# Input projection: the row loads of token blocks 0 and 1 ordered behind the last block's fifth row on ScalarE's queue

## The chip, the cores and the metric

The kernel runs on one core of a Trainium2 chip. The metric is the device time of one execution in microseconds (us); lower is better. Five engines work from queues of their own, each in order: TensorE (PE, matmuls), VectorE (DVE), ScalarE (ACT), GpSimd (POOL) and SyncE (SP). They wait for one another by semaphores. Transfers between memory and the core's buffers run on 16 DMA engines; a transfer is issued from the queue of SP, ACT or POOL, in order with what else stands in that queue.

## The reference, cut to what matters

One layer of a streaming encoder on 1024 prompt tokens and 8 x 16 sample tokens, in float32. What the change touches is its beginning:

```python
def rms_norm(x, g):
    xf = x.astype(jnp.float32)
    y = xf * lax.rsqrt(jnp.mean(xf * xf, axis=-1, keepdims=True) + EPS)
    return (y * g.astype(jnp.float32)).astype(x.dtype)

def hybrid_layer(x, p, ...):
    xn = rms_norm(x, norm_g)                       # 2048 wide
    u, g_pool, c_q, c_kv, k_r, g_mla = jnp.split(xn @ w_in, SPLIT_IDX, axis=-1)
    ...                                            # pooling mixer, latent attention
    h = x + jnp.concatenate([pool_out, mla_out], axis=-1) @ w_out
    gate = jax.nn.sigmoid(rms_norm(h, ple_norm_g) @ w_ple_gate + b_ple_gate)
    y = h + gate * (p @ w_ple)
```

## The kernel before, in words

The 1152 tokens are three blocks of TB = 384: blocks 0 and 1, and the "last block" (block 2). The 2048 features are 16 rows of 128; a row of one block is a tile of 128 partitions x 384 (192 KB). A value is split into a high and a low float32r part (`k.split`: ScalarE writes the high part, VectorE the low one), and a product is three matmuls: high x high, low x high, high x low (L175 to L177 in this phase; L77 to L79 in others).

The input projection (`phase1`) is a sum over two halves of the features. For the last block a product with one column of weights is plain: eight rows times three matmuls, 24. `EARLY` = 26 such columns come first and need only the last block's rows X0 to X7 (tiles x0 to x7 loaded by SyncE; X0h, X0l and so on are their two halves) and weights (`wraw`, split into `wh` and `wl`). The weight buffers are three deep before the split and five deep after it.

Meanwhile `row(c)` loads row c of blocks 0 and 1, for all 16 rows, as two transfers each on ScalarE's queue (32 in all), squares it on ScalarE and adds it to R on VectorE. Rows 0 to 7 go to tiles x0 to x7 (the buffers that the last block's rows leave), rows 8 to 15 in turn to two buffers xs. When R is whole, six small matmuls (L327, tile aux) and a chain on VectorE turn it into a factor per token, the rows are normalised (L371), and `first_operands` makes the operands 11, S1, S2, S3, S4, 12 and 22 from sums and differences of them. With these the products of blocks 0 and 1 run in pairs of columns with seven products instead of eight (`Quick.pair`): its intermediate results u2 (L210), u3 (L221) and q (L226) are made on VectorE. Between the pairs `second_operands` loads the rows of the second half (tiles a0 to a3), scales them (L464), forms their sums (L384 to L391) and stores them (tensor sums), all on SyncE's queue. After the second pair the shared rope key is projected (`key`, L438), with its own weights (wh_354).

The order in which each engine's instructions stand is not the order of the code: the tile framework plays the program through a cost model of its own when it is built, and gives each engine the order in which things came out there. `tc.issue_after(ins)` adds to this that what is written in its block stands behind `ins` on the engine of `ins`. So an edit at one place can move instructions far from it.

Of the kernel before, what the change touches and what calls it, by code (L numbers as in the profile page):

```python
# [8 lines left out]
AF = mybir.ActivationFunctionType  # L9
ALU = mybir.AluOpType  # L10
# [11 lines left out]
TB = 384  # L22
# [230 lines left out]
def phase1(k, sc):  # L253
# [4 lines left out]
    tc, nc, io = k.tc, k.nc, k.io  # L258
# [30 lines left out]
    def o_tile():  # L289
        return k.t(xp, [P, TB], "o", bufs=3)  # L290
# [10 lines left out]
    def last_block(c, j):  # L301

        i = 8 * c + j
        raw = (o_tile() if c else k.t(rp, [P, 2 * TB], f"x{j}"))[:, :TB]
        nc.sync.dma_start(raw, io["xT"][2][:, i, :])
        hl = [k.t(xp, [P, TB], f"X{j}{x}", F32R) for x in "hl"]
        k.split(hl[0][:], hl[1][:], raw, k.norm_g[:, i:i + 1])
        if c == 0:
            squares(R2, raw, raw)
        return hl  # L310

    begun = set()

    def squares(acc, raw, sq):

        if id(acc) not in begun:
            begun.add(id(acc))
            nc.scalar.activation(acc[:], raw, AF.Square)
        else:
            nc.scalar.activation(sq, raw, AF.Square)  # L320
            nc.vector.tensor_tensor(acc[:], acc[:], sq, ALU.add)
# [23 lines left out]
    raw = k.t(wp, [P, 8, P], "wraw", bufs=3)  # L345
    wn = [k.t(wp, [P, 8, P], f"w{x}", F32R, bufs=5) for x in "hl"]
    X = []
    for a, b in ((0, 1), (1, 2), (2, 4), (4, 8)):
        nc.sync.dma_start(raw[:, a:b, :], src[0][:, a:b, :])
        if a == 0:  # L350
            consts(k)
        k.split(wn[0][:, a:b], wn[1][:, a:b], raw[:, a:b])
        X += [last_block(0, j) for j in range(a, b)]
# [3 lines left out]
    def row(c):  # L357

        raw = k.t(rp, [P, 2 * TB], f"x{c}" if c < 8 else "xs", bufs=1 if c < 8 else 2)
        for t in range(2):  # L360
            nc.scalar.dma_start(raw[:, t * TB:(t + 1) * TB], io["xT"][t][:, c, :])
        squares(R, raw[:], (k.t(rp, [P, 2 * TB], "sq") if c < 8 else raw)[:])
        rows.append(raw)

# [34 lines left out]
    def square_rest(i):  # L399
        raw = o_tile()  # L400
        nc.sync.dma_start(raw[:], io["xT"][2][:, i, :])
        squares(R2, raw[:], raw[:])

    steps += [lambda c=c: row(c) for c in range(16)] + [norms, normalise]
    steps += [lambda j=j: first_operands(j) for j in range(4)]
    for i in range(EARLY):
# [95 lines left out]
    for n in OPS:  # L502
        for j in range(4):
            raw = k.t(ap, [P, TB], f"a{j}")
            nc.sync.dma_start(raw[:], sc["sums"][:, 4 * OPS.index(n) + j, :])
            put(n, j, raw[:])
    hs.close()
    X = [last_block(1, j) for j in range(8)]

    def prior(i, t):  # L510
# [1053 lines left out]
def layer(tc, io):  # L1564
    k = K(tc, io)
    with tc.tile_pool(name="dram", bufs=1, space=DRAM) as dp, tc.tile_pool(name="const", bufs=1) as cp:
        sc = scratch(dp, k)
        k.cp = cp
        first = phase1(k, sc)
        next(first)  # L1570
        shared = Shared(k)
# [110 lines left out]
```

## Time and profile before

| | us |
|---|---|
| median of 3 runs (lowest to highest) | 2288.55 (2285.35 to 2288.8) |
| the profiled execution, its own time | 2292.38 |
| its span, first to last instruction | 2290.6 |
| TensorE busy in the span | 2211.1 |
| VectorE busy | 1439.5 |
| ScalarE busy | 1004.0 |
| TensorE busy from 0 to 134 us | 123.04 |
| TensorE busy from 0 to 185 us | 165.12 |
| mean granted clock of TensorE | 0.987 |

TensorE is busy for 97% of the span, so the rows to look at are those in which it stands idle or works slowly. A row of the timeline has the start, the length, engine, line, operation, output<-inputs (without buffer numbers) and, in brackets, the idle time of that engine just before and what ended it. PEld is the weight load of a matmul; SPq and ACTq are the queues that issue transfers. A row of the waits has the waiting engine and line, who was waited for, the sum in us, how often, and the longest. A row of the stretches (from:to in us) has the busy time of PE, PEld, DVE, ACT and POOL with the number of instructions, the granted clock, the DMA engines' busy share and GB/s.

### The profile page before, as it was taken

To read this page: it belongs to the slowest core of one execution; us is meant where nothing else is said; L and a number is where in the kernel's file an instruction comes from. 1 tells how busy PE (TensorE), PEld (TensorE's weight loads), DVE (VectorE), ACT (ScalarE), POOL (GpSimd) and SP (SyncE) were. 2 spreads that over 40 slices of the span, in tenths; PEclk is the share of its full clock that TensorE was granted. 3 is DMA by queue.
4 is the path that set the end of the run, shared out by engine and by line. 5 is a ranking of instruction groups with operands and counts; after the bars stand their busy time and mean duration, and the time that the engine had idled before them with its cause. 6 is when DMAs were issued, how large, how long until landed. Compare 5 with 4: busy or idle time off the path is not lost.

```text
span 2290.6 us, 36006 instructions
## 1 busy us (share of the span) xinstructions
PE 2211.1 (97%) x12856; PEld 2154.0 (94%) x12856; DVE 1439.5 (63%) x3008; ACT 1004.0 (44%) x2229; POOL 410.8 (18%) x431
## 2 busy tenths in 40 slices
PE   8989999999898989989999899999999999999999
PEld 7989999999898989989998799999999999999998
DVE  6787776686777667768888765555553345344343
ACT  6533335443333467766666644343342233232232
POOL 0000000111222101034453532221002221111110
PEclk9999999999999999999999899999999999999999
DMA  9565336557766666473221754443263333222221
GB/s 303 178 225 169 125 125 213 166 161 192 190 185 179 216 206 179 130 240 99 93 84 53 241 179 152 128 154 122 85 198 112 101 121 110 86 94 96 85 87 64
DMA packets 241012, 339.24 MB, mean 148 GB/s; under 512 B 37729, under 2 KB 185313, under 8 KB 240833
## 3 DMA queue, kind: packets, MB, share of 16 engines
q1 hardware_dynamic: 217568, 290.77, 41.3%
q0 software_dynamic: 10880, 32.41, 4.4%
q10 hardware_dynamic: 12384, 13.77, 1.9%
q8 instruction: 101, 1.65, 0.3%
q14 instruction: 79, 0.64, 0.1%
HBM read 235.74 MB, written 101.12 MB: 147 GB/s over the span
## 4 chain that ended last, share of the span: by engine, by line
PE 66%; DMA 12%; DVE 9%; issue 8%; ACT 3%; POOL 2%; SPq 0%; ACTq 0%; DVEq 0%; POOLq 0%
PE mm L78 8%; PE mm L77 8%; PE mm L79 8%; PE mm L175 5%; PE mm L176 5%; PE mm L177 5%; PE f L77 3%; PE f L79 3%; PE f L78 3%; PE k L79 2%; PE k L78 2%; PE k L77 2%; DMA u<-u 1%; PE t L1215 1%; PE pb L77 1%
## 5 line engine op out<-in xcount | busy, mean ns | idle before, releaser
L68 ACT ACTIVATE wh<-wraw 128x1024 fp32r<-128x1024 f32 (+3 forms) x207 | 150.2, 729 | 146.3 <-PE mm L177 83.8
L69 DVE TENSOR_TENSOR wl<-wraw,wh 128x512 fp32r<-128x512 f32 (+3 forms) x205 | 172.0, 842 | 66.7 <-ACT wh L68 58.8
L1538 DVE TENSOR_TENSOR ev<-mm,R 128x384 f32<-128x384 f32 x48 | 26.7, 557 | 173.9 <-PE mm L79 170.0
L1539 ACT ACTIVATE ev<-ev,gains 128x384 f32<-128x384 f32 x48 | 29.4, 612 | 224.2 <-DVE ev L1538 124.4
L71 ACT ACTIVATE wh<-wraw,gains 128x128 fp32r<-128x128 f32 x256 | 82.1, 391 | 53.0 <-ACT wh L71 31.9
L72 DVE SCALAR_TENSOR_TENSOR wl<-wraw,gains,wh 128x128 fp32r<-128x128 f32 x256 | 88.0, 390 | 18.0 <-ACT wh L71 16.9
L77 PE MATMUL k<-wkh,ch 128*128 128x448 f32 x256 | 96.1, 376 | 3.2 <-ACT ch L68 2.7
L1216 ACT ACTIVATE pth<-t 128x512 fp32r<-128x512 f32 (+2 forms) x96 | 45.5, 485 | 119.7 <-PE t L1215 117.9
L68 ACT ACTIVATE wh<-wt 128x1024 fp32r<-128x1024 f32 x60 | 63.4, 1056 | 74.0 <-PE mm L177 48.5
L78 PE MATMUL k<-wkh,cl 128*128 128x448 f32 x256 | 94.5, 369 | 0.1
L79 PE MATMUL k<-wkl,ch 128*128 128x448 f32 x256 | 94.6, 369 | 0.0
L69 DVE TENSOR_TENSOR wl<-wt,wh 128x1024 fp32r<-128x1024 f32 x60 | 73.3, 1221 | 24.8 <-ACT wh L68 24.6
L79 PE MATMUL mm<-A2l,wh 128*128 128x384 f32 x256 | 86.0, 336 | 0.0
L77 PE MATMUL mm<-A2h,wh 128*128 128x384 f32 x256 | 86.0, 336 | 0.0
L78 PE MATMUL mm<-A2h,wl 128*128 128x384 f32 x256 | 86.0, 336 | 0.0
L77 PE MATMUL mm<-A0h,wh 128*128 128x384 f32 x256 | 85.8, 335 | 0.0
L79 PE MATMUL mm<-A0l,wh 128*128 128x384 f32 x256 | 85.7, 335 | 0.0
L78 PE MATMUL mm<-A1h,wl 128*128 128x384 f32 x256 | 85.7, 335 | 0.0
L78 PE MATMUL mm<-A0h,wl 128*128 128x384 f32 x256 | 85.7, 335 | 0.0
L77 PE MATMUL mm<-A1h,wh 128*128 128x384 f32 x256 | 85.5, 334 | 0.0
L79 PE MATMUL mm<-A1l,wh 128*128 128x384 f32 x256 | 85.5, 334 | 0.0
L1510 POOL TENSOR_TENSOR R<-R,sq 128x384 f32<-128x384 f32 x45 | 46.0, 1023 | 210.3 <-ACT sq L1509 210.3
(809 smaller groups left out, 7867.2 us busy)
## 6 DMA issues: line engine op xcount, KB each, us to landing
wraw<-w_in SPq DMA_DIRECT2D x89, 512.0 KB, 4.4
part<-o SPq DMA_DIRECT2D x93, 192.0 KB, 2.5
q<-part SPq DMA_DIRECT2D x93, 192.0 KB, 3.1
wraw<-w_out SPq DMA_DIRECT2D x64, 256.0 KB, 3.3
wraw<-w_ple_gate SPq DMA_DIRECT2D x64, 256.0 KB, 3.2
ple<-ev POOLq DMA_DIRECT2D x48, 192.0 KB, 2.9
fev<-xT SPq DMA_DIRECT2D x48, 192.0 KB, 2.5
hp<-fev SPq DMA_DIRECT2D x48, 192.0 KB, 2.1
```

The source lines that it names most:

```text
L68: nc.scalar.activation(hi, src, AF.Copy)
L69: eng.tensor_tensor(lo, src, hi, ALU.subtract)
L71: nc.scalar.activation(hi, src, AF.Copy, scale=scale)
L72: eng.scalar_tensor_tensor(lo, src, scale, hi, ALU.mult, ALU.subtract)
L77: mm(out, sh, mh, start=start, stop=False)
L78: mm(out, sl, mh, start=False, stop=False)
L79: self.last = mm(out, sh, ml, start=False, stop=stop)
L175: mm(ps, sh, xh[:], start=start and j == 0, stop=False, **kw)
L176: mm(ps, sl, xh[:], start=False, stop=False, **kw)
L177: self.k.last = mm(ps, sh, xl[:], start=False, stop=j == n - 1, **kw)
L1216: nc.scalar.activation(pth[:, :n, qq], tp[:, :n, :], AF.Copy)
L1510: nc.gpsimd.tensor_tensor(acc[t][:], acc[t][:], sq[:], ALU.add)
```

## The change

In `last_block` the split is written out, and the first half of it, the activation that writes the high part, is kept in a list `lead` for each of the eight rows. In `row` both loads are issued behind `lead[4]`, which is the activation of the fifth row, X4h.

```diff
         hl = [k.t(xp, [P, TB], f"X{j}{x}", F32R) for x in "hl"]
-        k.split(hl[0][:], hl[1][:], raw, k.norm_g[:, i:i + 1])
+        g = k.norm_g[:, i:i + 1]
+        hi = nc.scalar.activation(hl[0][:], raw, AF.Copy, scale=g)
+        nc.vector.scalar_tensor_tensor(hl[1][:], raw, g, hl[0][:], ALU.mult, ALU.subtract)
         if c == 0:
+            lead.append(hi)
             squares(R2, raw, raw)
...
-        for t in range(2):
-            nc.scalar.dma_start(raw[:, t * TB:(t + 1) * TB], io["xT"][t][:, c, :])
+        with tc.issue_after(lead[4].ins):
+            for t in range(2):
+                nc.scalar.dma_start(raw[:, t * TB:(t + 1) * TB], io["xT"][t][:, c, :])
```

ScalarE's queue from its first instructions, before (xs_118 and xs_119 are the buffers of rows 8 and 9, x0_54 and x1_57 the last block's first two rows):

```order
L361 DMA xs_118_424<-xT 128x384
L285 ACT_TABLE_LOAD
L285 ACTIVATE ones_46_123<-ones_46_123 128x128
L361 DMA xs_118_424<-xT 128x384
L68 ACTIVATE wh_50_129<-wraw_49_128 128x128
L361 DMA xs_119_429<-xT 128x384 x2
L320 ACTIVATE xs_118_424<-xs_118_424 128x768
L71 ACTIVATE X0h_55_139<-x0_54_137,gains_52_132 128x384
L318 ACTIVATE R2_48_127<-x0_54_137 128x384
L68 ACTIVATE wh_50_129<-wraw_49_128 128x128
L320 ACTIVATE xs_119_429<-xs_119_429 128x768
L71 ACTIVATE X1h_58_149<-x1_57_147,gains_52_132 128x384
```

And in the changed kernel, the same queue from the first split on:

```order
L308 ACTIVATE X0h_55_139<-x0_54_137,gains_52_132 128x384
L322 ACTIVATE R2_48_127<-x0_54_137 128x384
L68 ACTIVATE wh_50_129<-wraw_49_128 128x128
L308 ACTIVATE X1h_58_149<-x1_57_147,gains_52_132 128x384
L68 ACTIVATE wh_50_129<-wraw_49_128 128x256
L308 ACTIVATE X2h_61_160<-x2_60_158,gains_52_132 128x384
L308 ACTIVATE X3h_64_168<-x3_63_166,gains_52_132 128x384
L324 ACTIVATE x1_57_147<-x1_57_147 128x384
L68 ACTIVATE wh_50_129<-wraw_49_128 128x512
L324 ACTIVATE x2_60_158<-x2_60_158 128x384
L308 ACTIVATE X4h_67_179<-x4_66_177,gains_52_132 128x384
L366 DMA x0_82_241<-xT 128x384
```

The four loads of xs and the squares of them that stood ahead of X0h and X1h are gone from here; the first load of a row of blocks 0 and 1 is now x0_82, behind X4h. The xs loads stand 27 places further on, after those of x7, and ahead of the high half of the fifth column's weights (wh_106).

The order also differs from there to the second pair, on all of PE, DVE, ACT and SP, and again in the attention (PE's places 7026 to 7977 of 12822); everywhere else the five queues stand as before. VectorE's queue at the second pair's u3 (u3_351), before:

```order
L69 TENSOR_TENSOR wl_318_1407<-wraw_309_1387,wh_317_1406 128x512
L159 TENSOR_TENSOR wt_333_1500<-wraw_330_1494,wt_333_1500 128x512
L384 TENSOR_TENSOR as_561_2851<-a2_559_2841,a3_560_2842 128x384
L69 TENSOR_TENSOR wl_332_1497<-wraw_329_1492,wh_331_1496 128x1024
L297 TENSOR_TENSOR o_346_1575<-q_328_1490,o_345_1560 128x384
L297 TENSOR_TENSOR o_347_1579<-u2_323_1439,mm_322_1426 128x384
L391 TENSOR_TENSOR a2_559_2841<-a0_557_2839,a2_559_2841 128x384
L69 TENSOR_TENSOR wl_335_1504<-wt_333_1500,wh_334_1503 128x1024
L221 TENSOR_TENSOR u3_351_1629<-mm_341_1518,s1_342_1531 128x384
```

And in the changed kernel:

```order
L69 TENSOR_TENSOR wl_332_1497<-wraw_329_1492,wh_331_1496 128x1024
L391 TENSOR_TENSOR as_512_2561<-as_512_2561,a0_508_2549 128x384
L158 TENSOR_TENSOR wt_333_1500<-wraw_330_1494,wraw_329_1492 128x512
L469 SCALAR_TENSOR_TENSOR a3_560_2842<-a3_560_2842,gains_52_132,R_47_126 128x384
L394 TENSOR_TENSOR a1_509_2550<-a1_509_2550,as_512_2561 128x384
L159 TENSOR_TENSOR wt_333_1500<-wraw_330_1494,wt_333_1500 128x512
L221 TENSOR_TENSOR u3_351_1629<-mm_341_1518,s1_342_1531 128x384
L226 TENSOR_TENSOR q_352_1631<-mm_343_1533,u3_351_1629 128x384
L246 TENSOR_TENSOR u2_344_1546<-u2_344_1546,q_352_1631 128x384
L69 TENSOR_TENSOR wl_335_1504<-wt_333_1500,wh_334_1503 128x1024
```

u3_351 stands five instructions earlier: the work on a0_557, a2_559 and as_561 (second operands of the third group) and the split wl_335 have moved behind it.

More of the change, by code (lines that the diff above doesn't have):

```diff
@@ L312, in phase1 @@
     begun = set()
+    lead = []
     def squares(acc, raw, sq):
```

## The prediction

> **What bounds the kernel now.** I read first the page's busy shares and its chain of work that ended last.
>
> ```profile
> PE 2211.1 (97%) x12856; PEld 2154.0 (94%) x12856; DVE 1439.5 (63%) x3008; ACT 1004.0 (44%) x2229; POOL 410.8 (18%) x431
> PE 66%; DMA 12%; DVE 9%; issue 8%; ACT 3%; POOL 2%; SPq 0%; ACTq 0%; DVEq 0%; POOLq 0%
> ```
>
> TensorE is the bound: 2211.1 of 2290.6 us. An edit that adds no matmul can only win from the 79.5 us in which TensorE stood still, or from matmuls at a slow clock. So I asked for TensorE's waits in the stretches where the order of instructions changes. In the first 25 us:
>
> ```profile
> PE mm L175 <- ACT X0h L71: 6.2, 1, 6.2
> PE mm L175 <- ACT X1h L71: 2.3, 1, 2.3
> PE mm L175 <- ACT X5h L71: 2.0, 1, 2.0
> PE mm L176 <- DVE wl L69: 0.4, 1, 0.4
> ```
>
> 10.9 us, nearly all behind the high halves of the last block's rows on ScalarE. ScalarE's timeline (start, length, then in brackets the idle time before and what ended it) says why these are late:
>
> ```profile
> 4.72 0.84 ACT L320 ACTIVATE xs<-xs 128x768 f32<-128x768 f32 x1 [0.62 <-DMA xs<-xT]
> 5.54 0.62 ACT L71 ACTIVATE X0h<-x,gains 128x384 fp32r<-128x384 f32 x1
> 8.44 0.84 ACT L320 ACTIVATE xs<-xs 128x768 f32<-128x768 f32 x1 [1.66 <-DMA xs<-xT]
> 9.19 0.60 ACT L71 ACTIVATE X1h<-x,gains 128x384 fp32r<-128x384 f32 x1
> 15.28 0.84 ACT L318 ACTIVATE R<-x 128x768 f32<-128x768 f32 x1 [1.90 <-DMA x<-xT]
> 16.02 0.60 ACT L71 ACTIVATE X5h<-x,gains 128x384 fp32r<-128x384 f32 x1
> ```
>
> Each late half stands directly behind a square of a row of blocks 0 and 1 (xs twice, then R<-x), and two of the three squares waited over 1.6 us for their row. SyncE's queue is held too:
>
> ```profile
> SPq L305 <- DMA xs<-xT: 1.4, 1, 1.4
> 3.97 0.33 SPq L305 DMA_DIRECT2D x<-xT  x1
> x<-xT SPq DMA_DIRECT2D x8, 192.0 KB, 4.8
> ```
>
> The second row of the last block went out at 3.97 us, 1.4 us of that a wait for an xs load; such a row takes a median of 4.8 us to land. The other stretch whose order changes is that of the first pairs (125 to 185 us):
>
> ```profile
> PE mm L175 <- DVE u L221: 4.6, 1, 4.6
> PE mm L438 <- DVE wh L69: 3.6, 1, 3.6
> DVE a L464 <- DMA a<-xT: 5.6, 5, 2.5
> ```
>
> There VectorE is the bound. It waits in turn for the a loads of the second half's operands.
>
> **The change, part by part.** *Split written out* (L71 and L72 become L308 and L309): the same activation and the same scalar_tensor_tensor in the same order. Nothing.
>
> *Row loads behind the fifth row.* Before, six of the 32 issues stood ahead of X4h (four xs, two x0), and with them the three squares quoted. Now all of them come after X4h, the squares of xs after those of x1 to x6. X0h gains the 5.54 - 4.72 = 0.8 us of a square, X1h the wait of 2.3 us, X5h that of 2.0 us: 5.1 us. The lower end is set by the rows' own landing: issued at 3.97 - 1.4 = 2.6 us, the second row lands at 7.4 with the median, and X1h comes 9.19 - 7.4 = 1.8 us earlier; the same for X5h, 3.6 us in all. The upper end is 5.1 + 1.4 = 6.5 us, if SyncE's wait goes too and every later row moves up with it.
>
> What is late next are the weights. The moved loads meet them: four loads of 192 KB that had gone out first of all now lie on ScalarE's queue after x7, and the high half of the fifth column's weights (wh_106) stands behind four more issues in that in-order queue. Its cover before:
>
> ```profile
> 29.27 1.05 ACT L68 ACTIVATE wh<-wraw 128x1024 fp32r<-128x1024 f32 x1
> 30.35 1.22 DVE L69 TENSOR_TENSOR wl<-wraw,wh 128x1024 fp32r<-128x1024 f32 x1
> 34.03 0.33 PE L176 MATMUL mm<-X0h,wl 128*128 128x384 f32 x1
> 10.00:15.00 5.00, 4.65 (x12) 3.19 (x12) 4.37 (x9) 3.38 (x8) 0.00 (x0) 1.00 0.99 308
> ```
>
> The low half was done at 31.57 us and used at 34.03: 2.5 us of cover, with the DMA engines at 0.99 of their time (the last two columns are the DMA share and GB/s). TensorE wants these weights 5.1 us earlier. The path gets earlier too, since its buffers are freed earlier, but 768 KB at 308 GB/s is 2.6 us of transfer that now lies ahead of it. So 5.1 - 2.5 = 2.6 us must come from the earlier start; it lacks between 0 and 2.6. I take 0.6, near the lower end, because SyncE's own loads run alone for the first 10 us. **Start: 5.1 - 0.6 = 4.5 us, between 1.0 (3.6 - 2.6) and 6.5.**
>
> The Trainium skill, "DMA: Bandwidth & Descriptors", section "Issuing engines are not separate DMA queues", says that transfers issued by ScalarE and SyncE run on the same 16 engines and interleave. By that alone the 768 KB are only moved, and the start would be worth 5.1 - 2.6 = 2.5 us; the 0.99 above agrees with it.
>
> *The sum of squares R.* Its last addition moves later against TensorE's columns, and its six matmuls (L327) from the twelfth column to the thirteenth.
>
> ```profile
> 61.91 0.96 DVE L321 TENSOR_TENSOR R<-R,xs 128x768 f32<-128x768 f32 x1 [0.20 <-ACT xs L320]
> 66.26 1.23 PE aux L327 x12
> ```
>
> R was ready at 62.87 us and read at 66.26: 3.4 us of cover. TensorE comes 4.5 us sooner, but the reader stands 13 matmuls of 0.174 us, 2.3 us, later. Cover left if R keeps its time: 1.2 us. So nothing, and up to 2 us of loss if the loads fall behind.
>
> *The pairs.* This is the scheduler's doing, not the edit's: from 125 to 185 us four engines stand in another order. TensorE's longest wait is for the vector result u3_351, its next for the key weights wh_354.
>
> ```profile
> 154.17 1.22 DVE L69 TENSOR_TENSOR wl<-wraw,wh 128x1024 fp32r<-128x1024 f32 x1
> 155.31 0.55 DVE L297 TENSOR_TENSOR o<-q,o 128x384 f32<-128x384 f32 x1
> 157.84 0.55 DVE L221 TENSOR_TENSOR u<-mm,s 128x384 f32<-128x384 f32 x1
> 158.31 0.61 DVE L464 SCALAR_TENSOR_TENSOR a<-a,gains,R 128x384 f32<-128x384 f32 x1
> 158.84 0.55 DVE L386 TENSOR_TENSOR as<-as,a 128x384 f32<-128x384 f32 x1
> 167.29 0.69 DVE L69 TENSOR_TENSOR wh<-wraw,wh 128x512 fp32r<-128x512 f32 x1
> 171.75 0.62 DVE L464 SCALAR_TENSOR_TENSOR a<-a,gains,R 128x384 f32<-128x384 f32 x1 [2.51 <-DMA a<-xT]
> ```
>
> From the stretch's first L158 on, the new order has the same instructions ahead of u3_351 less five: two L464, L384, L391 and one weight split. By the distances between starts above (0.53, 0.47 and 1.14 us) that is 2 x 0.53 + 2 x 0.47 + 1.14 = 3.1 us. Ahead of wh_354 it has five fewer too: three L464, L386, L389, 3 x 0.53 + 2 x 0.47 = 2.5 us. The second decides when TensorE goes on, so work alone gives 2.5 us. The a loads that go later also take waits with them: 5.6 - 2.5 = 3.1 us of VectorE's waits for them lay ahead of wh_354. If all go it is 5.6 us, if half, 4.1. I take 4.0: the loads ahead of u3_351 are now two fewer of eleven, and on SyncE's queue the others stand behind fewer stores of sums. It can come out at nothing or below: all 16 operand groups still have to be done before the pair after the keys, so what is put off can be asked for at that pair, and a worse fit of SyncE's loads would cost another wait like the longest one, 4.6 us. **Pairs: 4.0 us, between -4 and +6.**
>
> *The attention stretch.* Between 1310 and 1460 us the scheduler's order differs again, with the same instructions.
>
> ```profile
> 1300.00:1350.00 50.00, 47.61 (x291) 44.20 (x290) 39.26 (x81) 31.67 (x71) 24.48 (x21) 0.98 0.79 254
> 1350.00:1400.00 50.00, 50.00 (x320) 48.48 (x319) 28.16 (x62) 20.79 (x45) 12.59 (x10) 1.00 0.44 136
> ```
>
> TensorE is busy 50.00 of 50 us from 1350 on, with VectorE at 28, so there is little to win or lose: 0, between +2.4 (the idle time of the first row) and -3. Everywhere else the four engines and GpSimd's queue stand as before, so a shift is carried to the end.
>
> **Sum.** 4.5 + 4.0 + 0 = 8.5 us. The profiled execution took 2292.38 us (span 2290.6), 3.8 above the median of the runs, 2288.55. The sum is made against its rows; I take it off the median: 2280.0 us, -0.37%. About 0.2% (4.6 us) is what a measurement of this kernel tells from no change.
>
> **The rivals.** *One of the two gains is eaten.* Either the weights behind the row loads take the start back to 1 us, or VectorE's order is worth nothing at the pairs because the work put off is wanted right after. Then 1.0 + 2.5 (VectorE's work alone) or 4.5 + 0, some 3 to 4.5 us, taken at 3.5: 2285. For it: the DMA share of 0.99 from 10 us. Against: after 21 us no wait of TensorE for weights is left to grow before the pairs. Chance 0.27; a third of it lies beyond 4.6 us.
>
> *Slower: VectorE stops at results of TensorE.* In the new order u2_323 (L210) stands ahead of three weight splits (wl_305, wl_307, wl_311), where it stood behind them, and the two results after it (u3_327, q_328) are moved forward too. Where VectorE comes to one before its product is done, all its work behind stands.
>
> ```profile
> 128.42 0.55 DVE L384 TENSOR_TENSOR as<-a,a 128x384 f32<-128x384 f32 x1
> 131.51 0.34 PE L177 MATMUL mm<-S_3l,wh 128*128 128x384 f32 x1
> ```
>
> In these rows VectorE comes to the place of u2_323 at 128.97 us, and the product ends at 131.85: 2.9 us lost on the engine that is the bound. If it loses as much at u3_327 and again at the next pair's u2_344, that is 8.7 us against 2.5 us of work saved, 6.2 us later at the key weights. With a start of 1.0 the kernel is 5.2 us slower: 2293.8. It decides from 2.5 + 4.5 = 7.0 us of such stops on, if the start brings what I forecast. Against it: by the time of u3_327 VectorE has three weight splits more behind it, so only the first stop is sure, and that one also lets the a loads come in, for which VectorE waited 3.1 us here before. Chance 0.09.
>
> *The clock rises within the first product.*
>
> ```profile
> 16.68 0.69 PE L175 MATMUL mm<-X5h,wh 128*128 128x384 f32 x1 [2.03 <-ACT X5h L71]
> 19.45 0.52 PE L177 MATMUL mm<-X7l,wh 128*128 128x384 f32 x1
> 19.77 0.52 PE L175 MATMUL mm<-X0h,wh 128*128 128x384 f32 x1
> 22.59 0.34 PE L176 MATMUL mm<-X2h,wl 128*128 128x384 f32 x1
> 22.76 0.33 PE L177 MATMUL mm<-X2l,wh 128*128 128x384 f32 x1
> ```
>
> Matmuls start 0.32 us apart at 19.5 us and 0.17 apart at 22.6, after TensorE had worked with pauses since 6.2. Without the pauses half of the 24 could run at the faster pace, 12 x 0.15 = 1.8 us, if the second product's weights are there; with SyncE's wait gone as well, 1.4, the sum is 8.5 + 3.2: 2276.8. The Trainium skill, "TensorE: Matmul & The Clock Gate", part 1, states about 3.4 us of sustained work for the full clock, and the trace's run without a wait from 16.68 to 19.77 us, 3.1 us, was still slow at its end, which does not contradict it. Chance 0.10.
>
> *The change does nothing that counts*: the X rows are late by their own transfers, and the pairs fall as before. 2288, chance 0.08.
>
> **How the numbers follow.** My forecast, 2280, has 0.46, with a range of its own from 2276 to 2284. Faster by over 0.2%: 0.46 + 0.10 + 0.27/3 = 0.65. Within: 0.18 + 0.08 = 0.26. Slower: 0.09. The range: at the low end the best of the start and of the pairs, 6.5 + 6 + 2.4 = 15, gives 2273.5, so 2273; at the high end the case of no effect, 2288, with a microsecond for the spread of runs, 2289.
>
> **What would show it.** Right: TensorE's waits for X1h and X5h gone and the second product begun near 15 us instead of 19.8; the wait at L221 below 2 us and the key matmuls (L438) beginning near 160 instead of 168; from 190 to 1300 us a constant shift. Wrong: a new wait of TensorE for wl or for R before 70 us, one for wl_305 at the pairs, or a wait for wl after the keys that gives the pairs back.

## The result, and the profile after

The changed kernel is slower. Median of 14 runs 2298.72 us (2289.4 to 2305.9) against 2289.93 us (2285.35 to 2296.33) for 14 runs of the kernel before: ratio 1.0033, 95% interval 1.0021 to 1.0045, so 4.8 to 10.3 us. I had forecast 2280. The profiled execution took 2298.22 us (span 2296.4).

```profile
PE 2215.5 (96%) x12856; PEld 2156.4 (94%) x12856; DVE 1441.2 (63%) x3008; ACT 1002.0 (44%) x2229; POOL 411.9 (18%) x431
```

No engine has more work: VectorE, ScalarE and GpSimd are within 2 us of before. TensorE's 4.4 us more of busy time go to the same 12856 matmuls, with a mean granted clock of 0.985 instead of 0.987. So again I read its waits, in the first 25 us and from 20 to 70 us, where before had only one of 0.4 us:

```profile
PE mm L175 <- ACT X0h L308: 4.9, 1, 4.9
PE mm L176 <- DVE wl L69: 1.8, 2, 1.0
PE mm L175 <- ACT X4h L308: 0.5, 1, 0.5
PE mm L175 <- ACT X3h L308: 0.5, 1, 0.5
PE mm L175 <- ACT X1h L308: 0.4, 1, 0.4
...
PE mm L176 <- DVE wl L69: 1.6, 2, 0.8
PE aux L331 <- DVE R L325: 1.5, 1, 1.5
PE mm L175 <- ACT wh L68: 0.7, 1, 0.7
```

The waits that the change was aimed at did go: X0h from 6.2 to 4.9, X1h from 2.3 to 0.4, X5h gone. In their place stand waits for weights (wl, wh) and one for R.

To see where time comes and goes, I took the start of the same matmul in both traces and subtracted: the *shift* (plus is later than before). This is worked out from the two timelines. For example the first key matmul, at 168.03 us before, starts at 170.54 here (shown below), a shift of +2.5.

| shift of TensorE at | 24 us | 60 us | 125 us | 190 us | from 1300 to 1470 us |
|---|---|---|---|---|---|
| changed kernel | -4.1 | -0.6 | +2.7 | +3.9 | +3.0 more |

The start is won at 24 us, given back by 60, and turned into a loss at R by 75; the pairs add 1.2 instead of bringing 4, and the attention adds 3.0. Of the 3.5 us given back by 60, 1.4 go at 22 us, where TensorE waits for the fourth column's weights, and 2.1 at 32 to 33 us, where it waits for the fifth column's. Together 2.7 + 1.2 + 3.0 = 6.9 us of the 7.6 that the ratio makes of 2289.93.

**The weights.** ScalarE's timeline after the changed loads, and its longest wait from 20 to 36 us:

```profile
22.14 1.39 ACTq L366 DMA_DIRECT2D x<-xT  x2
26.42 1.31 ACTq L366 DMA_DIRECT2D x<-xT  x2
28.31 0.85 ACT L324 ACTIVATE sq<-x 128x768 f32<-128x768 f32 x1 [4.46 <-DMA x<-xT]
30.93 1.04 ACT L68 ACTIVATE wh<-wraw 128x1024 fp32r<-128x1024 f32 x1
...
ACT sq L324 <- DMA x<-xT: 4.5, 1, 4.5
...
DMA to landing us min/median/max: 3.9/5.9/8.0
```

The row of 30.93 is the high half of the fifth column's weights. Its transfer went out at 21.00 us, and the last row says that no weight transfer of this stretch took over 8.0 us, so it had landed by 29.0 (that one took 6.2 us and landed at 27.2). But ScalarE's queue is in order. The program's own list of it shows what stood there (each row with what it waits for):

```
L366 DMA x_111_384<-xT 128x384 [waits DMAHW2_49,DVE_49]
L366 DMA x_111_384<-xT 128x384 [waits DMAHW3_49]
L366 DMA xs_424<-xT 128x384 [waits DMAHW5_49]
L324 ACTIVATE sq_289<-x_91_286 128x768 [waits DMAHW6_49,DVE_49]
L366 DMA xs_424<-xT 128x384 [waits DMAHW6_49]
L366 DMA xs_429<-xT 128x384 [waits DMAHW7_49]
L295 ACTIVATE o_298<-mm_261 128x384 [waits PE_49]
L366 DMA xs_429<-xT 128x384 [waits DMAHW0_49]
L324 ACTIVATE sq_295<-x_93_292 128x768 [waits DVE_49]
L68 ACTIVATE wh_349<-wraw_347 128x1024
```

Eight semaphores (DMAHW0 to 7) serve all transfers of SyncE and ScalarE in turn, and an issue waits until the earlier transfer on its semaphore has landed. The trace shows it: the four issues of 26.42 to 28.34 us began 0.02 to 0.08 us after landings at 26.34, 27.37, 27.81 and 28.32. The first row, x7's load, had to wait until 26.42, and with it the nine behind it. ScalarE did no work for 4.5 us. Before, the same activation ran at 29.27.

**R.** VectorE adds up R, and TensorE reads it (the first two rows are the additions of rows 2 and 8, the third is the last one):

```profile
29.19 0.96 DVE L325 TENSOR_TENSOR R<-R,sq 128x768 f32<-128x768 f32 x1 [3.95 <-ACT sq L324]
41.94 0.95 DVE L325 TENSOR_TENSOR R<-R,xs 128x768 f32<-128x768 f32 x1
...
67.89 0.96 DVE L325 TENSOR_TENSOR R<-R,xs 128x768 f32<-128x768 f32 x1 [0.39 <-ACT xs L324]
68.91 1.50 PE L331 MATMUL aux<-ones,R 128*128 128x1 f32 x12 [1.52 <-DVE R L325]
70.73 0.52 PE L177 MATMUL mm<-X1l,wh 128*128 128x384 f32 x1
71.05 0.52 PE L175 MATMUL mm<-X2h,wh 128*128 128x384 f32 x1
70.00:74.00 4.00, 4.00 (x16) 4.00 (x16) 3.52 (x14) 0.51 (x1) 0.00 (x0) 0.57 0.73 209
```

R's last addition came 6.0 us later than before (61.91), so the 3.4 us of cover were gone. It was late from row 2 on: that row's square is the sq_289 of the list above, it stood behind the issues that stopped there, and VectorE waited 4.0 us for it. Its addition came 3.5 us later than before (25.66), that of row 8 4.3 us later (37.65). After the wait of 1.5 us and the small matmuls that follow it, the granted clock is 0.57 from 70 to 74 us (the last row is that stretch): matmuls 0.32 us apart instead of 0.174. The 3.4 us at half clock cost 1.7 us on top of the wait.

**The pairs.** TensorE's waits from 125 to 200 us, then two waits of VectorE, and SyncE's issues; the first SyncE row is of before, all others of the changed kernel:

```profile
PE mm L443 <- DVE wh L69: 5.6, 1, 5.6
PE mm L175 <- DVE u L221: 1.9, 1, 1.9
PE mm L175 <- ACT wh L68: 1.3, 1, 1.3
PE mm L175 <- DVE u L210: 1.0, 1, 1.0
...
130.60 1.15 DVE L469 SCALAR_TENSOR_TENSOR a<-a,gains,R 128x384 f32<-128x384 f32 x2 [2.86 <-DMA a<-xT]
145.72 0.56 DVE L325 TENSOR_TENSOR R<-R,o 128x384 f32<-128x384 f32 x1 [2.92 <-ACT o L324]
...
170.54 0.69 PE L443 MATMUL mm<-11_0h,wh 128*128 128x384 f32 x1 [5.62 <-DVE wh L69]
```

```profile
120.26 1.87 SPq L463 DMA_DIRECT2D a<-xT  x4
```

```profile
118.45 8.92 SPq L298 DMA_DIRECT2D part<-o  x3
127.42 1.98 SPq L468 DMA_DIRECT2D a<-xT  x4
```

The wait at u3 fell from 4.6 to 1.9 as forecast. That for the key weights grew from 3.6 to 5.6. VectorE waited 2.9 us for the first a loads, which SyncE issued 7.2 us later than before, behind three stores, and 2.9 us for the square of a row of the last block. That the pairs add 1.2 us is no more than some runs with their old order show: e6, which starts as late, adds 1.2 as well, the two controls -0.5 and +0.5.

**The attention.** Before, TensorE's longest wait between 1300 and 1340 us was 1.3 us. Now:

```profile
1331.89 0.41 PE L77 MATMUL f<-M2h,wh 128*128 128x384 f32 x1 [3.18 <-DVE fev L1123]
...
1331.10 0.52 ACT L68 ACTIVATE M2h<-mraw 128x384 fp32r<-128x384 f32 x1 [1.93 <-DMA mraw<-mixp]
1331.21 0.54 DVE L1123 TENSOR_TENSOR fev<-f,fev 128x384 f32<-128x384 f32 x1
```

A product of the pooling mixer now stands 27 places earlier in TensorE's order, where two things that it waits for are not yet there: its operand M2h (ScalarE writes it from a late load, until 1331.62) and VectorE's fev, which the view names (until 1331.75). In e1, e2 and e8 below, the order of the attention differs from the changed kernel's at only 70 of TensorE's places; there this product finds both ready, and the stretch adds only 0.7 to 0.9 us. No run moves this product alone.

### The profile page after: what moved, and what is told of

It is laid out like the page before. It is cut to its first block, busy times and chain, and to the rows that moved or that the text cites. A ratio compares the mean times of both kernels' runs of the same rounds, so it can differ in the third digit from the quotient of the medians.

```text
span 2296.4 us, 36005 instructions
## 1 busy us (share of the span) xinstructions
PE 2215.5 (96%) x12856; PEld 2156.4 (94%) x12856; DVE 1441.2 (63%) x3008; ACT 1002.0 (44%) x2229; POOL 411.9 (18%) x431
## 4 chain that ended last, share of the span: by engine, by line
PE 65%; DMA 13%; DVE 8%; issue 8%; ACT 3%; POOL 1%; SPq 1%; ACTq 0%; DVEq 0%; POOLq 0%
PE mm L77 8%; PE mm L79 8%; PE mm L78 8%; PE mm L175 4%; PE mm L176 4%; PE mm L177 4%; PE f L77 3%; PE f L79 3%; PE f L78 3%; PE k L79 2%; PE k L78 2%; PE k L77 2%; DMA u<-u 2%; PE t L1220 1%; PE pb L77 1%
## 5 line engine op out<-in xcount | busy, mean ns | idle before, releaser
L1221 ACT ACTIVATE pth<-t 128x512 fp32r<-128x512 f32 (+2 forms) x96 | 45.6, 486 | 127.3 <-PE t L1220 126.3
L68 ACT ACTIVATE wh<-wt 128x1024 fp32r<-128x1024 f32 x60 | 63.4, 1057 | 84.4 <-PE mm L177 47.6
```

The lines of the kernel that those rows point to most:

```text
L68: nc.scalar.activation(hi, src, AF.Copy)
L1221: nc.scalar.activation(pth[:, :n, qq], tp[:, :n, :], AF.Copy)
```

## The experiments

Theory A was that the late row loads make the loss, at the start; theory B that the order of the pairs and of the attention, which the scheduler changed by itself, makes it. Later came theory Q (ScalarE's in-order queue stops at the issue of loads, ahead of the weights) against D (the DMA engines are full, the weights land late). Ratios are against runs of the kernel before on the same chip. The profiled executions of the control show what one profile can tell: against the earlier trace of before e5 lies at +0.2 us at 125 and +0.7 at 190, e16 between -0.6 and -1.6 up to there. So a shift of 1 us says little by itself. From 190 to 1300 us, with the order unchanged, it moved by -7.8 us and the other profiles by -13 to -1, so no shift is compared across that stretch.

| | at 24 | 60 | 125 | 190 | 1300 to 1470 | ratio (95% interval) |
|---|---|---|---|---|---|---|
| changed kernel | -4.1 | -0.6 | +2.7 | +3.9 | +3.0 | 1.0033 (1.0021 to 1.0045) |
| e14 changed again | -4.0 | +3.7 | +3.6 | +6.0 | +2.1 | not timed |
| e5 split only | +0.2 | +0.2 | +0.2 | +0.7 | +0.7 | 0.9998 (0.9985 to 1.0011) |
| e16 split only again | -1.6 | -1.1 | -0.6 | -1.1 | +0.4 | not timed |
| e6 new start, old rest | -4.2 | +4.2 | +4.2 | +5.3 | +0.3 | 1.0031 (1.002 to 1.0043) |
| e7 old start, new rest | -0.9 | -0.9 | -0.7 | +0.8 | +3.5 | 1.0012 (0.9998 to 1.0026) |
| e8 third xs buffer | -4.4 | +4.9 | +4.9 | +2.6 | +0.7 | 1.0034 (1.002 to 1.0048) |
| e9 weights ahead | -4.4 | -2.7 | +3.0 | +2.5 | +1.7 | 1.0021 (1.0005 to 1.0037) |
| e10 fewer weights | -4.3 | -2.7 | +5.4 | +2.5 | +0.9 | 1.0013 (0.9999 to 1.0028) |
| e11 rows on GpSimd | -1.1 | -1.1 | +1.3 | +1.2 | -0.8 | 1.0016 (1.0002 to 1.0031) |
| e12 rows 8, 9 on SyncE | -2.1 | -2.0 | -2.0 | -0.5 | -1.3 | 1.0022 (1.0007 to 1.0037) |
| e15 the same again | -2.6 | -2.6 | -2.6 | 0.0 | -0.6 | not timed |
| e13 R read later | -4.5 | -3.2 | -3.2 | -1.1 | -0.2 | 1.0009 (0.9997 to 1.0021) |

**e1 to e4: parts of the change, and other places for the loads.**

```diff
 e1: with tc.issue_after(lead[4].ins) if c in (8, 9) else ExitStack():   # around the two loads
 e2: with tc.issue_after(lead[4].ins) if c < 8 else ExitStack():
 e3: no issue_after around the loads, but
+        with tc.issue_after(lead[4].ins):
             squares(R, raw[:], ...)
 e4: lead[5] in place of lead[4]
```

> Only the four loads of rows 8 and 9 (xs) go behind X4h; the loads of x0 to x7 are free, and the order at the pairs is nearly that of before (8 of VectorE's places differ there). All shifts are of TensorE against the kernel before, at the same matmul. Theory A (late row loads: R and the weights come late and cost TensorE a wait and a fall of the clock): as in the changed kernel about -4 us at 24 us, but x0 to x2 are loaded earlier, so R's wait is smaller (0 to 1 us) and no fall of the clock follows: between -2 and +1 us at 125 us. Theory B (the new order of the pairs and of the attention makes the loss): the pairs give 0 since their order is that of before, the attention +1.5 as in the changed kernel; whole kernel within 0.1% of before.

> Only the loads of x0 to x7 go behind X4h; rows 8 and 9 are loaded first of all and squared ahead of X0h and X1h, as before. The order at the pairs and in the attention is the changed kernel's. Theory A: the gain at X0h and X1h (3 us) stays away, that at X5h (2 us) comes: -1 to -2 us at 24 us; R is late by less than 1 us, so -1 to +1 at 125 us. Theory B: the pairs lose 1 us or more and the attention 1.5, as in the changed kernel: +2 to +4 us from 125 us to the end, whatever the start does.

> No load is ordered; the squares of rows of blocks 0 and 1 on ScalarE go behind X4h instead. Loads leave as early as before; the order at the pairs is nearly that of before. Theory A: TensorE's waits for X0h, X1h and X5h shrink as in the changed kernel (-3 to -4 us at 24 us), and as the rows land as early as before R is not waited for: -3 to -4 us at 125 us, and the kernel 0.1 to 0.2% faster than before. Rival C (the DMA engines, full from 10 us on, set when weights are there, and give any gain at the start back): -3 to -4 at 24 us but within 1 us of before at 125 us, with waits of TensorE for wl between 24 and 35 us.

> All row loads behind the sixth row (X5h) instead of the fifth. The order at the pairs is near the changed kernel's, that of the attention is the one of before but for 14 places of TensorE. Theory A: row loads start later still, so at 125 us +2.7 us or more, up to +5; the attention adds 0 (from 1250 to 1460 us). Theory B: pairs as in the changed kernel, +1; the attention adds 0, so the whole is 1.5 us better than the changed kernel.

Measured: all four slower, 1.0049 (1.0031 to 1.0068), 1.0025 (1.0011 to 1.0039), 1.0025 (1.0009 to 1.0041) and 1.0022 (1.0006 to 1.0038). The shifts at 24 us are +3.2, -3.3, +0.7 and -4.3, at 125 us +3.9, +4.0, +10.6 and +4.1. So e1, expected at about -4 at 24 us, loses from the start (with the loads of x0 to x7 free again TensorE waited 2.3 us for X5h, and 3.2 us for weights), and neither half of the change alone is free. e3, in which no load was ordered, was expected to gain 3 to 4 us and had lost most at 125 us:

```profile
PE aux L331 <- DVE R L325: 6.0, 1, 6.0
```

Its squares of rows 8 and 9 came at 19.0 and 19.8 us instead of 4.7 and 8.4, their additions to R at 42.8 and 44.8 instead of 37.7 and 39.7, the next rows were loaded into their buffers from 45.3 instead of 38.6, and R's last addition came at 72.7. TensorE meets lateness anywhere on the way to R. e2 tells why R is late in the changed kernel: in e2 rows 8 and 9 were loaded first of all (from 0.7 us) and squared by 9, as before, and R was still late, by the same wait for row 2's square and with its last addition even after the changed kernel's:

```profile
29.55 0.96 DVE L325 TENSOR_TENSOR R<-R,sq 128x768 f32<-128x768 f32 x1 [4.60 <-ACT sq L324]
...
69.04 0.95 DVE L325 TENSOR_TENSOR R<-R,xs 128x768 f32<-128x768 f32 x1
```

So it is not the late loads of rows 8 and 9 that R waits for first. In e4 the attention keeps the order of before but for 14 places and adds +0.2 us between 1300 and 1470, which already speaks for B's part there.

**e5: the control.** The issue_after is taken out again; the order of every engine is that of before.

> The split is written out and nothing is ordered: every engine's order is that of before, so this is the kernel before again, and shows how far the same program differs from run to run. Both theories: ratio 1.000 within 0.1%; in its trace the shift of TensorE against the earlier trace of before within 1 us at 125 and at 190 us, while the stretch from 600 to 800 us, where the earlier runs moved by up to 5 us with an unchanged order, may move by as much.

0.9998: the split written out is nothing. The start and the pairs repeat within 0.7 us on another chip; on a third (e16) within 1.6 us, with -0.6 at 125 and -1.1 at 190 us, a little outside of what was expected.

**e6 and e7: one half's order each.** Edges at the end of the program give the engines a fixed order in two stretches:

```diff
         layer(tc, io)
+        hold(tc)     # for each pair a, b of neighbours in the other kernel's order of VectorE, ScalarE,
+                     # TensorE and SyncE at the pairs and in the attention:
+                     # tc.add_manual_dep(b, a.name, NoSync): b is issued behind a
```

> The changed kernel, with edges that give VectorE, ScalarE, TensorE and SyncE the order of before at the pairs (125 to 190 us) and in the attention. Theory A (the late row loads make the loss, at the start): start as in the changed kernel, +2 to +4 us at 125 us, then no more loss: +2 to +4 at 190 and 1460 us, and the whole 0.1 to 0.2% slower than before. Theory B (the order of the pairs and of the attention makes the loss): at 190 us 1 to 2 us less than the changed kernel, at 1460 us 3 us less, the whole within 0.1% of before.

> The kernel before, with edges that give the four engines the changed kernel's order at the pairs and in the attention; no load is moved. Theory A: 0 at 125 us and within 1 us of 0 at 190 us; the whole within 0.1% of before. Theory B: 0 at 125 us, +1 to +2 at 190, +2 to +4 at 1460 us; the whole 0.1 to 0.2% slower. My forecast for the pairs alone would make it 4 us faster at 190 us.

The new start alone costs 0.31%, nearly the whole. The new rest alone costs 0.12%, with an interval that just holds 1: by its profile +1.5 us in the pairs (from -0.7 to +0.8) and +3.5 in the attention. Theory A names the larger part, B a smaller one, and that in the attention: the 1.5 us in the pairs are no more than the 1.2 of e6 with the old order. My gain at the pairs was there and went again: in e7 the key weights came at 165.91 us, against 167.91 in e5, and the first key matmul at 166.65 against 168.65; at 190 us the two are level. What took the 2.0 us are a new wait of TensorE at the keys, 0.7 us for wl, and the clock behind them (waits of e7, then from 165 to 190 us e7 and, last, e5):

```profile
PE mm L438 <- DVE wh L69: 4.3, 1, 4.3
PE mm L438 <- DVE wl L425: 0.7, 1, 0.7
165.00:190.00 25.00, 22.70 (x112) 22.20 (x113) 14.21 (x24) 4.88 (x8) 0.00 (x0) 0.86 0.84 277
```

```profile
165.00:190.00 25.00, 21.35 (x113) 21.35 (x114) 13.44 (x22) 5.53 (x10) 0.00 (x0) 0.93 0.68 228
```

A clock of 0.86 instead of 0.93 over 25 us is 1.7 us less at full speed. In e6 the start's loss lay wholly at the weights, 1.8 us at the fourth column's and 6.6 at the fifth's:

```profile
30.55 0.85 ACT L324 ACTIVATE sq<-x 128x768 f32<-128x768 f32 x1 [6.44 <-DMA x<-xT]
33.71 1.04 ACT L68 ACTIVATE wh<-wraw 128x1024 fp32r<-128x1024 f32 x1
...
PE mm L175 <- ACT wh L68: 3.6, 2, 3.2
30.00:40.00 10.00, 6.27 (x23) 5.55 (x22) 6.97 (x7) 7.84 (x11) 0.00 (x0) 0.68 0.81 284
```

The same start as in the changed kernel's trace, but the weights' high half came at 33.7 instead of 30.9, TensorE waited 3.2 us for it, and its clock was 0.68 over the ten microseconds around it. That moved TensorE far enough back for R to be in time. The changed kernel, profiled again, came out like this too:

> The changed kernel, one more look. If its start varies from run to run, the waits for weights and for R at the start differ from the first profile by over 1 us each, with the shift at 125 us still between +1.5 and +6; a fall of the clock before 80 us in any case. At 1320 us again a wait of about 3 us ahead of f<-M2h.

There the wait for weights was 2.7 us, R was in time, and the shift at 125 us +3.6; the wait ahead of f<-M2h was 2.8 us. The loss moves between two waits, but it comes.

**e8: is R late for want of buffers?** `bufs=1 if c < 8 else 3` in place of 2.

> The changed kernel with three buffers xs instead of two, so that a row of the last eight can be loaded while two others wait for their square and sum. Theory A, in the form that R is late because the rows 8 to 15 pass through two buffers one after another: R is there when TensorE asks (no wait at the aux matmuls, no fall of the clock at 70 us), and the shift at 125 us is that left by the waits for weights, -1.5 to +0.5 us instead of +2.7. If R is late because the DMA engines are full, a third buffer changes nothing: a wait of 1 us or more for R and +2 or more at 125 us.

R's last addition came at 62.4 us instead of 67.9, so the two buffers do hold R back, and its wait was gone, though it was read 32 matmuls earlier. In this execution the weights were the late ones (3.5 us, with the clock at half from 35 to 42 us), and the expected shift of -1.5 to +0.5 came out as +4.9. e6 and e14, with two buffers, lost at the weights as well, so this run does not show what the third buffer is worth.

**e9, e10: the weights.** e9 adds edges from the high half of the sixth column's weights to the loads of x7 and of rows 8 and 9; e10 gives the columns 4 to 9, counted from 0, the weights of column 3, so their own weights are neither loaded nor split and the output is not the layer's.

```diff
 e9, on e6: + edges wh_115 -> the two loads each of x7, xs_118, xs_119 on ScalarE
 e10, on the changed kernel:
-        w, wn = wn, qk.hl(qk.raw(src[i + 1], 0)) if i + 1 < EARLY else None
+        w, wn = wn, wn if 4 <= i + 1 < 10 else qk.hl(qk.raw(src[i + 1], 0)) if i + 1 < EARLY else None
```

> New start and old rest as in e6, but on ScalarE the loads of x7 and of rows 8 and 9 (six issues) stand behind the high half of the sixth column's weights (wh_395), so that fewer issues stand ahead of the weights. Theory Q (ScalarE stops at the issue of a load until an earlier transfer has ended, and the weights' high half stands behind it): TensorE's wait for weights at 32 to 36 us falls from 3.7 us to under 1.5, and the shift at 60 us from +4.2 to between -3 and 0; but the last rows come 4 us later, so R is waited for at 70 us (2 to 6 us) and at 125 us it is between 0 and +6. Theory D (the DMA engines are full and the weights themselves land late): the wait at 32 to 36 us stays at 2.5 us or more.

> The changed kernel without the loads and splits of the weights of columns 4 to 9 (the fifth to the tenth): these columns use the tile of column 3 again, so 3 MB are not loaded and the result differs. If supply (transfers, and ScalarE's queue that issues and splits) is what gives the start's gain back, the gain stays: -3 to -5 us at 60 us and at 125 us, with no wait for weights after 24 us and none for R. If the gain is lost for another cause (TensorE's clock, VectorE's order), the shift at 125 us stays above 0.

TensorE's waits from 20 to 125 us in e9, ScalarE's row, and the same waits in e10:

```profile
PE aux L331 <- DVE R L325: 2.5, 1, 2.5
PE mm L176 <- DVE wl L69: 0.8, 1, 0.8
PE mm L175 <- ACT wh L68: 0.3, 1, 0.3
...
28.34 1.06 ACT L68 ACTIVATE wh<-wraw 128x1024 fp32r<-128x1024 f32 x1 [0.41 <-DMA wraw<-w_in]
```

```profile
PE aux L331 <- DVE R L325: 4.7, 1, 4.7
PE mm L176 <- DVE wl L69: 0.8, 1, 0.8
PE mm L175 <- ACT wh L68: 0.2, 1, 0.2
```

With six issues moved behind the weights, the fifth column's high half ran at 28.3 us, now behind its own transfer alone. The waits at 32 to 36 us are gone (the 0.8 and 0.3 lie at 22 us, at the fourth column's weights), and the shift stays at -2.7 to 60 us. This is Q, and not D: the engines were not less full, 0.93 of their time from 20 to 30 us against 0.88 in e6, and the transfer did not land earlier. In e9 it landed at 28.3 us and was used at once; in the changed kernel it landed at 27.2 and was used at 30.9, in e6 at 29.9 and 33.7. The stop had held the squares too: in e9 row 2's addition to R came at 26.1 us, against 31.4 in e6. Then R was waited for, because x7 itself was now loaded from 31.2 us and its addition, row 7's, came at 39.9. In e10 the weights part of the gain stayed too (-2.7 at 60 us), but R was waited for 4.7 us, against my expectation of none. Here the scheduler had put the six matmuls that read R at place 255 of TensorE's order instead of 293, 38 matmuls or 6.6 us earlier. R itself ended at 63.4 us, 5.5 earlier than in the changed kernel; at the old place it would have been in time. So e10 does not show a loss by another cause. Without these 3 MB and their splits on ScalarE and VectorE, R comes as early as with the third buffer of e8; which of the two, transfers or splits, does it is not separated.

**e11, e12: the row loads on other queues.**

```diff
 e11: nc.gpsimd.dma_start(raw[:, ...], ...)      # no issue_after around the loads; squares behind X4h
 e12: (nc.sync if c in (8, 9) else nc.gpsimd).dma_start(raw[:, ...], ...)   # squares behind X7h
 both: the rest held in the order of before
```

> Rest held in the order of before. The row loads of blocks 0 and 1 are issued by GpSimd, which has nothing else to do here, not delayed; only their squares stand behind X4h on ScalarE. Theory Q: ScalarE's queue no longer stops at issues, so the weights come in time; rows land as early as before: -2 to -4 us at 24, 60 and 125 us and no wait for weights or R; the whole 0.1 to 0.2% faster than before. Theory D: the bytes are the same, so whatever is gained at 24 us is given back by 60 us: within 1.5 us of 0 at 125 us.

> As e11, but rows 8 and 9 are loaded by SyncE behind the last block's rows and the weights of columns 1 to 3, and all squares of rows stand behind X7h. The X rows have the DMA engines to themselves as in the changed kernel: -4 us at 24 us. Theory Q: the rest of the gain stays as in e11, -3 to -4 us at 60 us; R in time if rows 8 and 9 have left the two buffers by 40 us: -3 to -4 at 125, the whole 0.15% faster than before. Theory D: waits for weights of 2 us or more between 28 and 40 us and 0 to +4 at 125 us.

> e12, one more look. If the start varies from run to run: a wait for weights or for R that the first profile did not have, and 0 us or more at 125 us. If not: -2 us at 125 us again, and its loss in time lies after 190 us.

In none of the three was there a wait for weights between 24 and 60 us, which is Q again. e11 won little at the start (X2h waited 1.9 us, with rows 8 and 9 loaded beside the X rows) and lost that at R. e12 is 2.0 and 2.6 us ahead at 125 us, without a wait for R, but level with before at 190 us: TensorE waits 2.6 us at the first pair's weights (wl), where before waited 0.7. In time both are slower than before, e12 by 0.07 to 0.37%. Nothing that I found up to 190 us explains that.

**e13: R read one column later.** Six more edges on e9: the six matmuls that read R stand 24 matmuls, one column, later.

> As e9 (weights ahead of the last six row loads, rest in the old order), and the six matmuls that read R stand 24 matmuls (one column, 4.2 us) later on TensorE. If weights and R are all that gives the start's gain back: no wait for weights at 32 us, none for R at 70 us, no fall of the clock there, and -2 to -3 us at 60 us and at 125 us; at 190 us -2 to +1, since the operands come later by the same column; the whole between 0.15% faster and 0.1% slower than before. If VectorE's work between R and the pairs was what R's lateness costs, a new wait of TensorE over 2 us comes between 125 and 150 us.

> The control of e5, one more look: within 0.5 us of the earlier profiles at 125 us and within 1 us at 190 us, with no wait of TensorE between 21 and 125 us.

TensorE's only wait from 20 to 125 us, and the stretch in which e9 had waited:

```profile
PE mm L176 <- DVE wl L69: 0.8, 1, 0.8
45.00:75.00 30.00, 30.00 (x179) 30.00 (x178) 17.77 (x26) 16.76 (x23) 0.00 (x0) 1.00 0.82 275
```

With both readers out of the way, TensorE is busy 30.00 of 30 us at full clock and the start's gain stands: -3.2 us from 30 to 125 us. So what gave the start's gain back after 30 us are the weights behind ScalarE's queue and R alone; the 1.3 us between -4.5 and -3.2 go at 22 us at the fourth column's weights, as in the other runs with this start. What is left is spent in the pairs, where TensorE waits 4.7, 2.5 and 1.1 us for VectorE's results and 2.4 for wl: -1.1 at 190 us, and 1.0009 in time. No version here is faster than before.

## Why the prediction was wrong, step by step

- *X0h, X1h, X5h (5.1 us, at least 3.6)*: right. -4.1 us at 24 us, and the second product began at 15.9 us instead of 19.8. The clock rose earlier with it, at 15.7 instead of 22.3 us by the change of the matmuls' spacing, as one rival had it; its extra 1.8 us did not show, since the second product then waited 1.0 us for its weights (wl), the condition that the rival had named.
- *Weights late (0.6 us)*: the step that failed first, by size. I had seen that the high half stands behind four more issues, and priced only their bytes (2.6 us at most). The fifth column's weights took 2.1 us in the first profile, 5.5 in e14 and 6.6 in e6, with the clock, and the fourth column's, for which the sum had no term, another 1.4 to 2.1. What I left out was that an issue itself can wait in ScalarE's queue for an earlier transfer (ScalarE stood 4.5 and 6.4 us) and holds all behind it; and that a new pause can bring half clock behind it. My own rows had shown such a wait: SyncE's issue of the second row stood 1.4 us for an xs load, and I did not ask the same of ScalarE's queue.
- *R (nothing, up to 2 us)*: failed. I let R keep its time and only asked how much sooner TensorE comes. But the same stop held the squares: row 2's addition came 3.5 us late and the last one 6.0, and 1.5 + 1.7 us were lost. That rows 8 and 9 were loaded at 28 instead of 1 us is not the cause by itself, since e2 loaded them first and had R later still; that the last rows go through two buffers adds to it (e8). e9 and e13 show what R's reader costs: 2.5 us of wait with R read in place, none with R read a column later. Both signs that I had named for being wrong before 70 us came, a wait for wl and one for R.
- *Pairs (4.0 us)*: the work was counted right, what lies around it was not. From its first L158 of the stretch to wh_354 VectorE took 43.2 us in e7 against 45.7 in e5, 2.5 us less (both worked out from its timeline). I had let another 1.5 us of its waits go with the moved loads; in the changed kernel its idle gaps there grew, from 5.5 to 6.7 us in sum. It also entered the stretch at 126.3 us instead of 121.8, after a late R, so wh_354 came 2.5 us later than before, just the start's loss. And the two pauses, 4.6 and 3.6 us, became one long one ahead of the keys (5.6) and a short one at u3 (1.9), with 6.8 us of half clock behind the long one, for which I had no term.
- *Attention (0, down to -3)*: came out at the bad end: 3.0, 2.1 and 3.5 us in the three profiles with the changed kernel's order (the first, e14, e7), against -1.3 to +1.7 in the eight with the old one (e5, e6, e9, e11 to e13, e15, e16). That TensorE was busy 50.00 of 50 us from 1350 on was true and told nothing of the 50 us ahead of that, where f<-M2h waited 2.8 to 3.2 us in these three profiles.
- *The rivals.* The slower case had a chance of 0.09, and it came for another reason: VectorE stood idle ahead of none of the results that I had named (it made u2_323 at 135.53 us without a pause), and what it lost in the pairs were its waits for the a loads and for a square. That one gain is eaten (2285) was the nearest; both were, and the start gave back more than it had brought. The sum by the rule of the Trainium skill, "DMA: Bandwidth & Descriptors", section "Issuing engines are not separate DMA queues", 2.5 us for the start instead of 4.5, lay nearer to the result than mine, yet by that sum too the start would have won; in e9 a mere change of order brought the weights' high half 2.6 us forward (28.3 instead of 30.9) with the same bytes, so the loss was one of the queue.

What stays open: why e11 and e12 are slower in time than their profiles up to 190 us make them. What makes them slower would lie after 190 us, where each profile differs from the next by more than the effect; whether the stores that GpSimd issues there take part was not tried. It is open too which of its two inputs holds f<-M2h, and why the same order loses at the weights in one execution and at R in another.

## What to carry to other kernels

Price a moved load by everything that stands behind its issue on an in-order queue, and by the buffers that it frees for the next one, not by its bytes. Where an engine is fed with little cover, here 2.5 us at the weights and 3.4 at R, a gain ahead of it is soon taken back there, unless what feeds it or its reader is moved too: e13 kept 3.2 us to 125 us only after six issues and the six readers of R had been moved. When an edit makes a scheduler reorder stages far away, hold their order with edges before the edit is judged; here that order alone measured 0.12% slower (-0.02 to 0.26%).

## What was not expected of the hardware

A short wait of TensorE can be followed by a slow clock if the work behind it is light: in the changed kernel 1.5 us for R, then 1.5 us of one-column matmuls, and the clock was half for 3.4 us. At the same place it fell after 0.9 us of wait in e2 and 0.55 in e11 (0.63 from 66 to 70 us there), but not after 0.6 in e1 (1.00 from 66 to 74 us), so the length of the wait alone does not decide it. The same small matmuls without a wait (before, and e13 at 68.78 us) left the clock at 1.00, and so did waits of 1.0 and 1.9 us that were followed by full products (the changed kernel, at 156 and 160 us). And the same order of the start lost mainly at the weights in two executions (e6, e14) and at R in one.
